# Float32 mixer and MoE layer: convolution sums in PSUM, low parts of weights on GpSimd, fewer native float32 chunks

## The chip, the core and the metric

The kernel runs on one core of one Trainium2 chip. The metric is device time in microseconds (us) of one execution. A core has five engines that the profile names PE (TensorE, matrix products), DVE (VectorE), ACT (ScalarE), POOL (GpSimd) and SP (SyncE, which here only issues DMAs). Every engine works through its own queue of instructions in order, and waits on semaphores for the others.

## The reference

One layer for a sequence of T = 256 tokens, D = 1024 channels, all float32. The first part mixes tokens, the second is a mixture of experts.

```
z = h @ w_in + b_in                        # 1024 x 6144: six blocks of 1024 columns
a_val, a_gate, sgu, g_a, g_b = split(z)    # sgu holds two blocks, u and v
ya = a_val * sigmoid(a_gate)
ya = causal_depthwise_conv(ya, 31 taps)    # every channel by itself
ya = silu(layer_norm(ya)) @ w_a + b_a
u, v = split(gelu(sgu))
yb = spatial_gating(u, layer_norm(v)) @ w_b + b_b
m  = sigmoid(g_a) * ya + sigmoid(g_b) * yb
out = m @ w_out + b_out                    # then residual, layer norm, modulation
y  = moe(h2)                               # top 4 of 32 experts, clamped SwiGLU, D -> 2*1024 -> D
```

The modulation rows (shift, scale, gate) come from c @ w_mod.

## The kernel before

**Part 1, the mixer (0 to about 316 us of the span).** Nine weight blocks of 1024 x 1024 go through PE one after the other: the block of a_gate, of a_val, V, U, G_b, G_a (columns of w_in), then w_b, w_a and w_out. A block is four chunks of 256 rows (one DMA of 1 MB each, issued by SP two chunks ahead), a chunk is two halves of 128 rows. A chunk is multiplied in one of two ways. A *native* chunk is multiplied as float32: 16 matmuls in the program, 32 in the trace. A *split* chunk is split into hi + lo: ACT casts the raw half to the rounded format fp32r (hi, L146), DVE subtracts (lo = raw - hi, L147), and PE multiplies hi by hi, hi by lo and lo by hi (L428 to L430): 48 matmuls. NAT_V, NAT_U, NAT_G, ... say which chunks of a block are native; N_LO = 6 buffers hold the lo halves of all blocks in turn.

**The convolution.** Each of the eight channel blocks n takes 31 taps. The first (L514) writes the product with its coefficient and the bias to cT[:, n] in SBUF, each of the other 30 (L516, SCALAR_TENSOR_TENSOR on 128 x 256 float32) reads that sum, adds one product and writes it back. That makes 248 DVE instructions. They are put into the background queue bgq in groups of four; bg_step (L408) takes groups out of it behind each chunk until their costs (0.33 each tap) have used a budget, BUD. Behind the convolution in the same queue stand the four steps of its layer norm (lna_mean, lna_var, lna_out twice: L600 to L617), whose result is split again (cahi, calo, L117/L118) and is the right-hand side of the w_a block.

**The order of the engines' queues.** Up to the chain behind w_out the framework's scheduler orders each engine's instructions by its own estimate of when they are ready, so that a budget or a cost that changes moves instructions. In the order that results DVE works on two channel blocks in turn, one tap of n, one of n + 1, as long as two are open.

**Around it.** macc and sacc (L250) are sums of modulation rows on DVE. sgb (L627) is the gate times the result of the w_b block, read from PSUM. The w_out block and its chain (L749 on: residual, layer norm, router, selection) lead to **part 2, the MoE**: 30 jobs, each an expert's weights streamed once.

**PSUM.** [...] The pool big holds three tiles of two banks, msp two of one.

Of the kernel before, what the change touches and what calls it, by code (L numbers as in the profile page):

```python
# [68 lines left out]
BUD = (7.2, 2.2)  # L69
# [6 lines left out]
def kernel(ctx, tc, a, out):  # L76
# [27 lines left out]
    def BIG():  # L104
        return big.tile([P, D], F32, name=nm("big"), tag="big")
# [60 lines left out]
    def push_block(key, w, c0, native):  # L166
        seq[key] = len(chunks)
        for ci in range(4):
            chunks.append(Chunk(lambda ci=ci: load_rows2(w, c0, ci), ci in native))

    for b, nat in ((1, ()), (0, ()), (3, NAT_V), (2, NAT_U), (5, NAT_G), (4, NAT_G)):
        push_block(("in", b), a["w_in"][0], b * D, nat)
    push_block("b", a["w_b"][0], 0, NAT_B)
    push_block("a", a["w_a"][0], 0, NAT_A)
    push_block("out", a["w_out"][0], 0, NAT_O)
# [173 lines left out]
    xT = [BIG(), BIG()]  # L349
# [6 lines left out]
    with tc.manual_schedule(engines={ET.DVE}):  # L356
# [23 lines left out]
        for g in range(2):  # L380
            pcol = MS()
            for w in range(2):
                for i in range(4):
# [4 lines left out]
            k4 = slice(g * 4, g * 4 + 4)
            ve.tensor_tensor(mcol[:, g, 0], pv[:, 0], par[:, k4, C_MOD], op=ALU.add)
            ve.scalar_tensor_tensor(mcol[:, g, 1], pv[:, 1], 1.0, par[:, k4, C_MOD + 1], op0=ALU.add, op1=ALU.add)  # L390
            for i in range(4):
                k = g * 4 + i
                src = xT[g][:, i * T:(i + 1) * T]
# [20 lines left out]
    def gemm_T(base, af, ahi, alo):  # L414
        accs = [BIG(), BIG()]
        for ci in range(4):
            ck = chunk(base + ci)
            for k2 in range(2):
                k = 2 * ci + k2
                for n in range(KC):  # L420
                    o = accs[n // 4][:, (n % 4) * T:(n % 4 + 1) * T]
# [86 lines left out]

    cT = sg

    def conv(n, t0, t1):
# [858 lines left out]
    undone = []  # L1370
    for j in range(NSTATIC + 1):
# [132 lines left out]
```

## Time and profile before

| | us |
|---|---|
| median of 3 runs | 1273.22 (1271.09 to 1273.25) |
| profiled execution | 1268.86 |
| its span, first to last instruction | 1267.0 |
| PE busy in the span | 1123.8 (89%) |
| DVE busy | 484.7 (38%) |
| ACT busy | 205.7 (16%) |
| POOL busy | 55.5 (4%) |
| DMA, mean over the span | 354 GB/s |

Times in rows are microseconds from the start of the span, and the name of an operation's tile says whose result it is: a name before the arrow is written, those behind it are read. A row with a count (x19) is a run of equal instructions, and its length goes from the first one's start to the last one's end. An instruction's record lasts somewhat longer than the distance to the next one, since they overlap. In brackets stands how long the engine was idle before, and whose work it waited for.

### The profile page before, as it was taken

What the parts mean: (1) busy time and instruction counts of PE and PEld (TensorE: products, weight loads), DVE (VectorE), ACT (ScalarE), POOL (GpSimd) and SP (SyncE); (2) the same over time, 40 slices, a digit from 0 to 9 for tenths busy, and PEclk for the clock granted to TensorE, in tenths of its full rate; (3) what the DMA queues carried; (4) which work ended last, traced back from release to release, by engine and by line L of the source; (5) the groups of instructions that cost most, each with busy time, mean ns of one, the idle gap of its engine ahead of it and who ended that gap; (6) DMA issues with size and microseconds to landing.
All of it is one profiled execution on the core that took longest, in us unless ns stands there. A gap on an engine that the chain in (4) does not pass through costs nothing. (4 is left out here: it accounts for less than half of the span.)

```text
span 1267.0 us, 14367 instructions
## 1 busy us (share of the span) xinstructions
PE 1123.8 (89%) x5454; PEld 548.3 (43%) x5454; DVE 484.7 (38%) x926; ACT 205.7 (16%) x344; POOL 55.5 (4%) x185
## 2 busy tenths in 40 slices
PE   1999999998999989999997999899888986998672
PEld 1998898876434334324331343334222321332110
DVE  6799999976321410321222113121121211132124
ACT  1533234533202001000110020011000100011000
POOL 6000000000200001000010010000000000000000
PEclk9999999999999999999998999899889988999676
DMA  9984346685897998999999999999999999999993
GB/s 367 368 334 134 116 151 223 231 306 204 349 418 293 383 418 330 375 399 404 377 417 417 417 403 404 416 417 416 416 417 417 416 417 418 417 417 417 417 414 111
DMA packets 84312, 449.13 MB, mean 354 GB/s; under 512 B 7377, under 2 KB 7417, under 8 KB 51424
## 3 DMA queue, kind: packets, MB, share of 16 engines
q1 hardware_dynamic: 82672, 443.84, 87.8%
q0 software_dynamic: 1552, 4.15, 0.9%
q8 instruction: 50, 0.82, 0.3%
q14 instruction: 38, 0.31, 0.1%
HBM read 446.92 MB, written 1.05 MB: 354 GB/s over the span
## 5 line engine op out<-in xcount | busy, mean ns | idle before, releaser
L1138 PE MATMUL big<-raw,S 128*32 128x512 f32 (+1 forms) x1600 | 279.0, 631 | 30.3 <-DMA raw<-in_w_gu_dram 30.3
L1149 PE MATMUL big<-raw,S 128*128 128x512 f32 x384 | 172.2, 602 | 0.0
L1314 DVE TENSOR_TENSOR ob<-big,g2c 64x512 f32<-64x512 f32 x48 | 33.0, 688 | 361.8 <-PE big L1289 253.1
L1138 PEld LDWEIGHTS big<-raw,S 128*32 128x32 f32 (+1 forms) x1600 | 63.3, 122 | 202.7 <-issue 128.8
L1149 PEld LDWEIGHTS big<-raw,S 128*128 128x128 f32 x384 | 71.9, 192 | 90.4 <-issue 89.3
L1289 PE MATMUL big<-raw,aT 128*32 128x512 f32 x512 | 75.9, 706 | 30.5 <-DMA raw<-in_w_dn_dram 29.2
L516 DVE SCALAR_TENSOR_TENSOR sg<-ya,par,sg 128x256 f32<-128x256 f32 x240 | 100.0, 470 | 0.6
L1280 PE MATMUL big<-raw,aT 128*128 128x512 f32 x192 | 87.0, 601 | 0.9 <-DMA raw<-in_w_dn_dram 0.9
L426 PE MATMUL big<-hT,raw 128*128 128x256 f32 x384 | 85.5, 379 | 0.0
L1342 PE MATMUL ms<-ob,ohT 128*128 128x512 f32 x144 | 76.8, 640 | 5.9 <-DVE gt L1182 3.2
L1334 DVE TENSOR_TENSOR y<-y,ms 128x512 f32<-128x512 f32 x72 | 48.9, 685 | 81.8 <-PE ms L1342 81.7
L426 PEld LDWEIGHTS big<-hT,raw 128*128 128x128 f32 x384 | 71.9, 190 | 9.5 <-issue 0.5
L1138 PE MATMUL big<-raw,aT 128*64 128x512 f32 x256 | 65.1, 621 | 4.2 <-DMA raw<-in_w_dn_dram 4.1
L147 DVE TENSOR_TENSOR lo<-raw,hi 128x1024 fp32r<-128x1024 f32 x46 | 55.2, 1216 | 9.5 <-ACT hi L146 6.4
L1172 ACT COPY g<-big 128x512 f32<-128x512 f32 x16 | 9.4, 585 | 302.1 <-PE big L1138 302.1
L1280 PEld LDWEIGHTS big<-raw,aT 128*128 128x128 f32 x192 | 35.2, 190 | 52.4 <-issue 50.6
L146 ACT CAST hi<-raw 128x1024 fp32r<-128x1024 f32 x46 | 46.3, 1051 | 59.1 <-DMA raw<-in_w_in_dram 17.3
L430 PE MATMUL big<-hThi,lo 128*128 128x256 f32 x192 | 55.0, 288 | 0.8 <-DVE lo L147 0.8
L428 PE MATMUL big<-hThi,hi 128*128 128x256 f32 x192 | 55.7, 291 | 0.0
L429 PE MATMUL big<-hTlo,hi 128*128 128x256 f32 x192 | 55.0, 287 | 0.1
L1289 PEld LDWEIGHTS big<-raw,aT 128*32 128x32 f32 x512 | 13.9, 118 | 87.5 <-DMA raw<-in_w_dn_dram 59.3
L1182 DVE TENSOR_TENSOR gt<-ms,bcols 128x256 f32<-128x256 f32 (+1 forms) x46 | 22.6, 491 | 75.0 <-PE ms L1208 75.0
(327 smaller groups left out, 1185.5 us busy)
## 6 DMA issues: line engine op xcount, KB each, us to landing
raw<-in_w_gu_dram SPq DMA_DIRECT2D x240, 1024.0 KB, 17.2
raw<-in_w_dn_dram SPq DMA_DIRECT2D x120, 1024.0 KB, 16.6
raw<-in_w_mod_dram SPq DMA_DIRECT2D x24, 1024.0 KB, 7.6
raw<-in_w_in_dram SPq DMA_DIRECT2D x24, 1024.0 KB, 7.1
raw<-in_w_b_dram SPq DMA_DIRECT2D x4, 1024.0 KB, 5.0
raw<-in_w_a_dram SPq DMA_DIRECT2D x4, 1024.0 KB, 5.0
raw<-in_w_out_dram SPq DMA_DIRECT2D x4, 1024.0 KB, 9.0
x<-in_x_dram SPq DMA_DIRECT2D x1, 1024.0 KB, 8.3
```

The costliest lines, as they stand in the source:

```text
L147: ve.tensor_tensor(c.lo[q], src, f(c.hi[q]), op=ALU.subtract)
L426: pe.matmul(o, lhsT=ck.raw[:, k2 * D + n * P:k2 * D + (n + 1) * P], rhs=af[:, k], start=b0, stop=b1)
L428: pe.matmul(o, lhsT=ck.hi[k2][:, s], rhs=ahi[:, k], start=b0, stop=False)
L429: pe.matmul(o, lhsT=ck.hi[k2][:, s], rhs=alo[:, k], start=False, stop=False)
L430: pe.matmul(o, lhsT=ck.lo[k2][:, s], rhs=ahi[:, k], start=False, stop=b1)
L516: ve.scalar_tensor_tensor(cT[:, n], ya[:, n, t:t + T], bcol(n, t), cT[:, n], op0=ALU.mult, op1=ALU.add)
L1138: pe.matmul(out_[q * n:(q + 1) * n], lhsT=S, rhs=raw[:, w0(q):w0(q) + 512], start=first_, stop=last_)
L1149: pe.matmul(job.ps[h][:, n * 512:(n + 1) * 512], lhsT=S[:, k, 0:P], rhs=raw[:, h * D + n * 512:h * D + (n + 1) * 512], start=f0, stop=f1)
L1280: pe.matmul(job.pd[0][:, n * 512:(n + 1) * 512], lhsT=job.aT[:, k, 0:P], rhs=raw[:, k2 * D + n * 512:k2 * D + (n + 1) * 512], start=f0, st ...
L1289: pe.matmul(job.pd[0][q * 32:(q + 1) * 32, 0:512], lhsT=job.aT[:, k, 0:32], rhs=raw[:, k2 * D + h * 512:k2 * D + (h + 1) * 512], start=ci ...
L1334: ve.tensor_tensor(yy, yy, box[0], op=ALU.add)
L1342: pe.matmul(box[0], lhsT=w()[r, t * P:(t + 1) * P], rhs=o(n)[r], start=i == 0, stop=i == len(parts_) - 1)
```

## The change

1. Of V, U, G_b and G_a one chunk each stays native (chunk 1), where three were: eight chunks more are split.
2. The lo halves of V, U, G_b, G_a and w_b are subtracted by GpSimd. Those of the first two blocks, of w_a and of w_out stay on DVE.
3. The sums of the convolution stand in a PSUM tile csum of one bank, [128, 2, 256]: channel block n uses half n % 2. After tap 31 ACT copies the half to cT in SBUF (L528).
4. Part 1 uses five single banks (zbp), one for csum and two of msp; the pool big is opened before the MoE.
5. The budget is three numbers, the cost of a tap 0.4.
6. The second half of the gate row's sum is added right before the MoE, and no longer in its first units.

Line numbers move: taps L514/L516 to L524/L526, lo L147 to L153, hi L146 to L152, sgb L627 to L639, modulation sums L250 to L257, layer norm L603 to L615.

```
-NAT_V = (1, 2, 3)
-NAT_U = (1, 2, 3)
-NAT_G = (0, 1, 3)
+NAT_V = (1,)
+NAT_U = (1,)
+NAT_G = (1,)
...
-BUD = (7.2, 2.2)
+BUD = (6.6, 5.0, 2.2)
...
-    big = ctx.enter_context(tc.tile_pool(name="big", bufs=3, space=PSUM))
     msp = ctx.enter_context(tc.tile_pool(name="msp", bufs=2, space=PSUM))
+    banks = ctx.enter_context(ExitStack())
+    zbp = banks.enter_context(tc.tile_pool(name="zbp", bufs=5, space=PSUM))
+    cvp = banks.enter_context(tc.tile_pool(name="cvp", bufs=1, space=PSUM))
...
-        ve.tensor_tensor(c.lo[q], src, f(c.hi[q]), op=ALU.subtract)
+        c.eng.tensor_tensor(c.lo[q], src, f(c.hi[q]), op=ALU.subtract)
...
+    for b, nat, eng in ((1, (), ve), (0, (), ve), (3, NAT_V, gp), (2, NAT_U, gp), (5, NAT_G, gp), (4, NAT_G, gp)):
+        push_block(("in", b), a["w_in"][0], b * D, nat, eng)
+    push_block("b", a["w_b"][0], 0, NAT_B, gp)
+    push_block("a", a["w_a"][0], 0, NAT_A, ve)
+    push_block("out", a["w_out"][0], 0, NAT_O, ve)
...
     def gemm_T(base, af, ahi, alo):
-        accs = [BIG(), BIG()]
+        accs = [ZB() for i in range(4)]
...
-            bg_step(BUD[0] if ck.native else BUD[1])
+            bg_step(BUD[0] if ck.native else BUD[1] if ck.eng is gp else BUD[2])
...
     cT = sg
+    csum = cvp.tile([P, 2, T], F32, name="csum")
 
     def conv(n, t0, t1):
         for t in range(t0, t1):
+            o = csum[:, n % 2]
             if t == 0:
-                ve.tensor_scalar(cT[:, n], ya[:, n, 0:T], bcol(n, 0), bcol(n, C_CONVB), op0=ALU.mult, op1=ALU.add)
+                ve.tensor_scalar(o, ya[:, n, 0:T], bcol(n, 0), bcol(n, C_CONVB), op0=ALU.mult, op1=ALU.add)
             else:
-                ve.scalar_tensor_tensor(cT[:, n], ya[:, n, t:t + T], bcol(n, t), cT[:, n], op0=ALU.mult, op1=ALU.add)
+                ve.scalar_tensor_tensor(o, ya[:, n, t:t + T], bcol(n, t), o, op0=ALU.mult, op1=ALU.add)
+            if t == TAPS - 1:
+                sc.copy(cT[:, n], o)
...
+    for n in range(2):
+        ns = slice(n * 512, (n + 1) * 512)
+        ve.tensor_tensor(g2c[:, ns], g2c[:, ns], pg2[n], op=ALU.add)
+    banks.close()
+    bigs.append(ctx.enter_context(tc.tile_pool(name="big", bufs=3, space=PSUM)))
...
-    def gate_unit():
-        return [lambda: ve.tensor_tensor(g2c, g2c, pg2, op=ALU.add)]
```

At the start of the convolution DVE's queue reads so before; ya is the gated input, macc a modulation sum, sg_604 the sums:

```order
L507 SCALAR_TENSOR_TENSOR ya<-big_614,par,sg_604 128x256 x4
L514 TENSOR_SCALAR sg_604<-ya,par 128x256
L250 SCALAR_TENSOR_TENSOR macc_415<-raw_848,condT,macc_415 128x2048
L516 SCALAR_TENSOR_TENSOR sg_604<-ya,par,sg_604 128x256
L514 TENSOR_SCALAR sg_604<-ya,par 128x256
L516 SCALAR_TENSOR_TENSOR sg_604<-ya,par,sg_604 128x256 x19
```

Two first taps stand almost side by side there, so two channel blocks are open. In the changed kernel the queue of the same place (bs_899 is a bias row of the spatial gating) reads:

```order
L524 TENSOR_SCALAR csum<-ya,par 128x256
L526 SCALAR_TENSOR_TENSOR csum<-ya,par,csum 128x256
L257 SCALAR_TENSOR_TENSOR macc_422<-raw_857,condT,macc_422 128x2048
L526 SCALAR_TENSOR_TENSOR csum<-ya,par,csum 128x256 x17
L552 SCALAR_TENSOR_TENSOR bs_899<-ms_901,par,bs_899 128x128 x4
L552 SCALAR_TENSOR_TENSOR bs_899<-ms_907,par,bs_899 128x128 x4
L526 SCALAR_TENSOR_TENSOR csum<-ya,par,csum 128x256 x12
L524 TENSOR_SCALAR csum<-ya,par 128x256
L526 SCALAR_TENSOR_TENSOR csum<-ya,par,csum 128x256 x13
```

There 30 taps stand between one first tap (L524) and the next: one channel block is open at a time, all through the convolution.

At the convolution's end DVE's queue reads so before; lo_18.. are halves of w_a, ms_1804 the mean of the layer norm, sgb the gate times the w_b block:

```order
L147 TENSOR_TENSOR lo_1889<-raw_1886,hi_1888 128x1024
L516 SCALAR_TENSOR_TENSOR sg_604<-ya,par,sg_604 128x256 x4
L147 TENSOR_TENSOR lo_1893<-raw_1886,hi_1892 128x1024
L516 SCALAR_TENSOR_TENSOR sg_604<-ya,par,sg_604 128x256
L250 SCALAR_TENSOR_TENSOR sacc_2096<-raw_2099,condT,sacc_2096 128x1024
L603 TENSOR_TENSOR sg_604<-sg_604,ms_1804 128x1024 x2
L147 TENSOR_TENSOR lo_1954<-raw_1951,hi_1953 128x1024
```

In the changed kernel the last part of the convolution, from the last sgb on, reads:

```order
L639 SCALAR_TENSOR_TENSOR sgb_1812<-zb_2093,par,sgb_1812 128x256
L526 SCALAR_TENSOR_TENSOR csum<-ya,par,csum 128x256
L153 TENSOR_TENSOR lo_2397<-raw_2390,hi_2396 128x1024
L526 SCALAR_TENSOR_TENSOR csum<-ya,par,csum 128x256
L257 SCALAR_TENSOR_TENSOR sacc_2448<-raw_2513,condT,sacc_2448 128x1024
```

and its very end:

```order
L257 SCALAR_TENSOR_TENSOR sacc_2448<-raw_2629,condT,sacc_2448 128x1024
L526 SCALAR_TENSOR_TENSOR csum<-ya,par,csum 128x256 x10
L524 TENSOR_SCALAR csum<-ya,par 128x256
L526 SCALAR_TENSOR_TENSOR csum<-ya,par,csum 128x256 x30
L615 TENSOR_TENSOR sg_611<-sg_611,ms_2152 128x1024 x2
```

The eight sgb, which stood behind the layer norm before, now stand between taps with the last 60 of the 248 taps behind the first of them, and all eight sums of sacc and six low halves of w_a stand ahead of the last tap, where one macc and four halves of w_a stood.

## Rows read from the trace of the kernel before

**Rows 1.** The page's costliest group: xcount | busy us, mean ns | idle, releaser.

```profile
L1138 PE MATMUL big<-raw,S 128*32 128x512 f32 (+1 forms) x1600 | 279.0, 631 | 30.3 <-DMA raw<-in_w_gu_dram 30.3
```

**Rows 2.** Windows: length, busy PE, PEld, DVE, ACT, POOL, PEclk, DMA, GB/s.

```profile
39.05:43.67 4.62, 4.56 (x20) 4.27 (x21) 4.62 (x8) 4.48 (x7) 0.00 (x0) 1.00 1.04 376
43.67:48.29 4.62, 4.62 (x42) 4.62 (x42) 4.62 (x7) 2.35 (x5) 0.00 (x0) 1.00 0.94 335
125.00:150.00 25.00, 25.00 (x123) 22.19 (x122) 25.00 (x65) 6.70 (x12) 0.00 (x0) 1.00 0.38 119
350.00:375.00 25.00, 25.00 (x98) 9.81 (x96) 8.79 (x18) 1.84 (x3) 0.00 (x0) 1.00 1.01 418
```

**Rows 3.** PE timeline: start us, length us, operation, xcount [idle before <-releaser].

```profile
125.18 20.88 PE L426 MATMUL big<-hT,raw 128*128 128x256 f32 x96
...
238.24 1.98 PE L492 MATMUL big<-bg,ones 1*128 1x512 f32 x4
...
244.47 0.39 PE L429 MATMUL big<-calo,hi 128*128 128x256 f32 x1 [0.39 <-DVE calo L118]
...
266.13 1.45 PE L473 MATMUL ms<-sacc,ones 128*128 128x512 f32 x3
...
282.97 1.04 PE L671 MATMUL ms<-ident,sc 128*128 128x128 f32 x8
...
286.53 0.48 PE L694 MATMUL big<-hi,mhi 128*128 128x512 f32 x1
```

**Rows 4.** DVE timeline, the convolution's start and its end.

```profile
83.94 3.22 DVE L507 SCALAR_TENSOR_TENSOR ya<-big,par,sg 128x256 f32<-128x256 f32 x8 [2.10 <-PE big L430]
...
90.38 7.60 DVE L516 SCALAR_TENSOR_TENSOR sg<-ya,par,sg 128x256 f32<-128x256 f32 x19
...
208.34 5.15 DVE L516 SCALAR_TENSOR_TENSOR sg<-ya,par,sg 128x256 f32<-128x256 f32 x10
...
224.18 0.48 DVE L516 SCALAR_TENSOR_TENSOR sg<-ya,par,sg 128x256 f32<-128x256 f32 x1
224.58 1.28 DVE L250 SCALAR_TENSOR_TENSOR sacc<-raw,condT,sacc 128x1024 f32<-128x1024 f32 x1
```

**Rows 5.** One DVE group: line, op, tiles, shapes, xcount | busy, mean ns.

```profile
L572 DVE SCALAR_TENSOR_TENSOR m<-ms,par,bs 128x256 f32<-128x256 f32 x8 | 3.7, 466 | 0.0
```

**Rows 6.** DVE timeline, the layer norm behind the convolution.

```profile
232.76 1.23 DVE L147 TENSOR_TENSOR lo<-raw,hi 128x1024 fp32r<-128x1024 f32 x1 [2.31 <-PE big L430]
233.91 1.75 DVE L611 RECIPROCAL rstd<-rstd 128x256 f32<-128x256 f32 x1
235.57 1.18 DVE L147 TENSOR_TENSOR lo<-raw,hi 128x1024 fp32r<-128x1024 f32 x1
...
238.93 3.22 DVE L627 SCALAR_TENSOR_TENSOR sgb<-big,par,sgb 128x256 f32<-128x256 f32 x8
...
243.20 1.22 DVE L118 TENSOR_TENSOR calo<-sg,cahi 128x1024 fp32r<-128x1024 f32 x1
```

**Rows 7.** ACT timeline, the layer norm behind the convolution.

```profile
231.98 0.48 ACT L610 ACTIVATE rstd<-ms,eps 128x256 f32<-128x256 f32 x1 [1.47 <-PE ms L609]
...
240.39 1.03 ACT L117 CAST cahi<-sg 128x1024 fp32r<-128x1024 f32 x1
```

**Rows 8.** POOL groups by form, whole span.

```profile
L925 POOL TENSOR_SCALAR oh<-iota_s,P 128x32 fp32r<-128x32 f32 x32 | 11.1, 366 | 264.7 <-PE ms L948 262.8 <-DVE P L903 1.9
L925 POOL TENSOR_SCALAR oh<-iota_s,P 128x128 fp32r<-128x128 f32 x10 | 6.1, 613 | 0.0
...
L464 POOL MEMSET sacc<- 128x1024 f32 x1 | 1.0, 959 | 61.5 <-PE ms L569 61.5
...
L295 POOL TENSOR_SCALAR lowr<-pio 128x1 f32<-128x1 f32 x1 | 0.2, 233 | 0.0
```

**Rows 9.** Timeline at the start of the span, DVE and POOL.

```profile
15.21 9.51 DVE L250 SCALAR_TENSOR_TENSOR macc<-raw,condT,macc 128x2048 f32<-128x2048 f32 x4
15.30 2.35 POOL L297 TENSOR_SCALAR lowr<-tgt 128x1 f32<-128x1 f32 x1
```

More of the change, by code (lines that the diff above doesn't have):

```diff
@@ L104, in BIG, with ZB @@
     def BIG():
-        return big.tile([P, D], F32, name=nm("big"), tag="big")
+        return bigs[0].tile([P, D], F32, name=nm("big"), tag="big")
+    def ZB():
+        return zbp.tile([P, 512], F32, name=nm("zb"), tag="zb")
     def MS():
@@ L133, with __init__ @@
     class Chunk:
-        def __init__(self, load, native):
-            self.load, self.native = load, native
+        def __init__(self, load, native, eng):
+            self.load, self.native, self.eng = load, native, eng
             self.raw, self.hi, self.lo = None, [], []
@@ L164, with push_block @@
     seq = {}
-    def push_block(key, w, c0, native):
+    def push_block(key, w, c0, native, eng):
         seq[key] = len(chunks)
         for ci in range(4):
[L169 to L175, printed above, removed]
+            chunks.append(Chunk(lambda ci=ci: load_rows2(w, c0, ci), ci in native, eng))
+    for b, nat, eng in ((1, (), ve), (0, (), ve), (3, NAT_V, gp), (2, NAT_U, gp), (5, NAT_G, gp), (4, NAT_G, gp)):
[3 more added lines that the diff above has]
+    push_block("out", a["w_out"][0], 0, NAT_O, ve)
     regs = {}
@@ L347, in part_of @@
         return t_.rearrange("p (w c) -> p w c", w=2)[:, :, g * 512:(g + 1) * 512]
-    xT = [BIG(), BIG()]
+    xT = [ZB() for i in range(4)]
     mcol = const.tile([P, 2, 2, 4], F32, name="mcol")
@@ L392 @@
                 k = g * 4 + i
-                src = xT[g][:, i * T:(i + 1) * T]
+                src = xT[k // 2][:, i % 2 * T:(i % 2 + 1) * T]
                 scale, shift = mcol[:, g, 1, i:i + 1], mcol[:, g, 0, i:i + 1]
@@ L420, in gemm_T @@
                 for n in range(KC):
-                    o = accs[n // 4][:, (n % 4) * T:(n % 4 + 1) * T]
+                    o = accs[n // 2][:, (n % 2) * T:(n % 2 + 1) * T]
                     s = slice(n * P, (n + 1) * P)
@@ L430, in gemm_T @@
                         pe.matmul(o, lhsT=ck.lo[k2][:, s], rhs=ahi[:, k], start=False, stop=b1)
-            bg_step(BUD[0] if ck.native else BUD[1])
-        return [accs[n // 4][:, (n % 4) * T:(n % 4 + 1) * T] for n in range(KC)]
+            bg_step(BUD[0] if ck.native else BUD[1] if ck.eng is gp else BUD[2])
+        return [accs[n // 2][:, (n % 2) * T:(n % 2 + 1) * T] for n in range(KC)]
     def z_block(b):
@@ L476, in mod_g2 @@
     def mod_g2(c0, c1):
-        pg = BIG()
+        pg = [ZB(), ZB()]
         steps = []
@@ L491, in step @@
         def step(i, lhsT, w, n):
-            pe.matmul(pg[:, n * 512:(n + 1) * 512], lhsT=lhsT, rhs=w, start=i < 2, stop=i >= len(steps) - 2)
+            pe.matmul(pg[n], lhsT=lhsT, rhs=w, start=i < 2, stop=i >= len(steps) - 2)
         return [lambda i=i, s=s: step(i, *s) for i, s in enumerate(steps)], pg
@@ L520 @@
             t1 = min(t0 + 4, TAPS)
-            bgq.append((0.33 * (t1 - t0), lambda n=n, t0=t0, t1=t1: conv(n, t0, t1)))
+            bgq.append((0.4 * (t1 - t0), lambda n=n, t0=t0, t1=t1: conv(n, t0, t1)))
     wsr = A8([P, KC, P], name="wsr")
@@ L631 @@
         fn()
-    sc.copy(g2c, pg)
+    for n in range(2):
+        sc.copy(g2c[:, n * 512:(n + 1) * 512], pg[n])
     z = gemm_T(seq["a"], cT, ca_hi, ca_lo)
@@ L679, in prepare_router @@
             sc.mul(wr[:, k], wr[:, k], modc[:, 0, k:k + 1])
-    yo = [BIG(), BIG()]
+    yo = [[ZB(), ZB()] for t in range(NT)]
     def out_mm(t, ci, k2, n):
@@ L687, in out_mm @@
         k = 2 * ci + k2
-        o = yo[t][:, n * 512:(n + 1) * 512]
+        o = yo[t][n]
         s = slice(n * 512, (n + 1) * 512)
@@ L835 @@
     c_norm(0)
-    pl = BIG()
+    pl = ZB()
     c_transpose(0)
@@ L897 @@
     c_lo(1, 0)
-    pj = BIG()
+    pj = ZB()
     for t in range(NT):
@@ L930 @@
     c_lo(1, 1)
+    for n in range(2):
+        ns = slice(n * 512, (n + 1) * 512)
+        ve.tensor_tensor(g2c[:, ns], g2c[:, ns], pg2[n], op=ALU.add)
+    banks.close()
+    bigs.append(ctx.enter_context(tc.tile_pool(name="big", bufs=3, space=PSUM)))
     class Job:
@@ L1376 @@
         else:
-            waiting += [tail_unit(), bias_unit(0), bias_unit(1), weight_unit(), gate_unit()] + start_units()
+            waiting += [tail_unit(), bias_unit(0), bias_unit(1), weight_unit()] + start_units()
             first_gather = gather(0)
```

5 lines of the change are left out of this document (3 added, 2 removed).

## The prediction

> **What bounds the kernel now.** I read busy time by stretch first, then the timelines of PE and DVE where part 1 ends, then the costliest groups. From 350 to 375 us the DMA queues are busy all the time at 418 GB/s [rows 2], and PE's costliest group, in the MoE, is idle 30.3 us waiting for weights [rows 1]. The MoE is thus a stream of fixed length that starts when part 1 hands over; what part 1 wins or loses goes into the total about one for one. In part 1 PE and DVE are both full: 125 to 150 us has 25.00 us of each [rows 2], and neither can be relieved alone. Where they meet is the w_a block. It starts at 244.47 after a wait for DVE's calo and runs to 266.13 [rows 3]; calo comes from the layer norm, and that from the last tap, which stands at 224.18 and ends, by the start of the next instruction, at 224.58 [rows 4]. So the question is when, in the changed kernel, the last tap ends. I call that time E.
>
> **PE's side.** 96 matmuls (three native chunks) take 20.88 us [rows 3], 6.96 each. The w_a block has four split chunks, of which 190 of 192 matmuls stand between 244.47 and 266.13 [rows 3]: 5.47 a chunk. Eight chunks that change from one to the other save 8 x 1.49 = 11.9 us of PE. Where does that put the end of w_b? The blocks V to w_b start when a_val's does not hold PE any more, at 83.9 [rows 4], and w_b ended at 238.2, where the next work of PE starts [rows 3]: 154.3 us, of which 12 x 6.96 + 8 x 5.47 = 127.3 are chunks and 27.0 other work and waits. Of these I drop 12 (an estimate: the 32 small matmuls of the layer norm, now behind w_b, and waits for DVE's low halves). New: 4 x 6.96 + 16 x 5.47 = 115.4, plus 15, so w_b ends at about 214.
>
> **DVE's side, taken away.** 12 of the 16 low halves that stood between 83.9 and E leave DVE. One takes 1.15 us (232.76 to 233.91 [rows 6]): -13.8.
>
> **DVE's side, added.** Two more halves of w_a stand ahead of E (+2.3), eight sums sacc at 1.2 (the first at 224.58 has 1.28, the next starts a little before it ends [rows 4]; +9.6) and eight sgb, 3.22 together [rows 6]. Then the taps themselves. Each tap reads the sum that the tap before wrote. With two channel blocks in turn, 19 taps took 7.60 us, a distance of (7.60 - 0.48)/18 = 0.396; where one block alone was left, ten took 5.15, a distance of 0.52 [rows 4]. So a tap that directly follows the tap it depends on pays 0.124 us. In the changed order only one block is open at a time. The reason is csum: two blocks have two halves, but the first tap of the next block also waits for ACT's copy of the last one. I count 188 taps right behind their predecessor, where some 17 were: 171 x 0.124 = +21.2. This is the largest term, and rests on the delay being the same for a sum in PSUM, which no row shows. Bounds: nothing at all (0.396, PSUM hides it) and twice the delay (0.64); I take the row's 0.52. The seven changes of block wait for an ACT copy: an ACT operation of that size out of PSUM takes 0.48 [rows 7]; with both semaphores 0.6, six times beyond what other work covers, +3.6 (0 to 8, when ACT is in the middle of a 1.03 us cast [rows 7]). The sum is +26.1: by its own work DVE would reach E at 224.6 + 26.1 = 250.7.
>
> A PSUM operand as such costs nothing that rows show: the taps' 0.48 in SBUF [rows 4] stands beside 466 ns for an operation of the same kind and size that reads PSUM [rows 5]. [...]
>
> **What PE adds to this.** The first sgb reads w_b's result, so it can't start before 214, and behind it stand 60 taps, 44 of them chained: 44 x 0.52 + 16 x 0.396 + 8 sgb (3.2) + 6 sacc (7.2) + one half (1.15) + one change (0.6) = 41.4. So E is at least about 255, and the two ways agree to 5 us: PE ends w_b early, stands idle for about 42 us, and waits for DVE. I take 254, that is 29.4 us later than before.
>
> **GpSimd's low halves.** 32 halves, 128 x 1024, two inputs. GpSimd's one-hot takes 366 ns at 32 columns and 613 at 128 [rows 8]: 2.57 ns a column, 2.9 us a half. Bounds: a MEMSET of that size, 0.96 [rows 8], and twice the slope for two inputs, 5.7. A block has six halves, 17.4 us against 23.4 of PE (6.96 + 3 x 5.47), so PE doesn't wait until a half takes 3.9.
>
> **DVE and GpSimd beside each other.** While DVE ran 2048-column sums with two SBUF inputs back to back, a GpSimd operation on one column took 2.35 us, the length of one such sum [rows 9], and 0.23 for the same operation elsewhere [rows 8]. GpSimd thus waits for DVE; the other direction has no row. Some 11 instructions of DVE with two SBUF inputs stand among GpSimd's halves. If each waits half a half (1.45) with GpSimd busy three quarters of the time, that is 12 us on DVE's side; all of GpSimd's halves in a bad order could make it 20. DVE has about 4 us to spare against the 214 of w_b, so between 0 and 16 reach E; I take 6, near half. The taps themselves have one SBUF input now. [...]
>
> **From E to the end.** Before, 244.47 - 224.58 = 19.9 us lay between E and w_a. Two low halves stood ahead of the reciprocal and behind it; without them the reciprocal starts at 232.5, when the root is there [rows 7], not at 233.9, and the next step 1.1 us sooner [rows 6]. calo could follow ACT's cast, at 241.4 [rows 7], not at 243.2, behind the sgb and a half [rows 6]. That is 1.4 + 1.1 + 1.8 = 4.3, less 0.9 for small ACT copies that are ordered between: -3.4. So w_a starts at 254 + 16.5 = 270.5, 26.0 later. PE then comes from idleness: in its first 4.62 us of work it did 20 matmuls, in the next 42, with a granted clock of 1.00 in both records [rows 2]; half of 4.62 is lost, +2.3. The transposes and small matmuls between the two halves of w_out (282.97 to 286.53 [rows 3]) fall into PE's idle time now: -3.6. The sum of the gate row's second half adds 0.3 on DVE ahead of the MoE, and three matmuls of the modulation right behind w_a (L473, 1.45 [rows 3]) move ahead of it, which gives back 0.4, since DVE works there anyway. PSUM in single banks and the budgets cost nothing by themselves: they act through the order.
>
> **Sum.** +26.0 + 2.3 - 3.6 + 0.3 - 0.4 + 6 = +30.6 on the profiled execution's 1268.86, so 1299.5. The median of the runs is 4.4 us above that execution; so 1303 against 1273.22. The 11.9 us that PE saves are in none of these terms, because PE waits.
>
> **Rivals.**
> 1. *The chain's delay is hidden in PSUM* (0.396 everywhere). For it: nothing in the rows but that the store is another. DVE then reaches the first sgb before w_b ends, and E is 214 + 41.4 - 44 x 0.124 = 250, later if ports cost; the rest stays: about 10 us less, 1293. Chance 0.13.
> 2. *PSUM makes the chain longer* (0.64). E moves by 188 x 0.12 = 22, of which 4 were to spare: about 1320. For it: the sum goes out to another memory and comes back; against it: reading PSUM cost nothing extra [rows 5]. [...] Chance 0.12.
> 3. *GpSimd starves PE*, at 4.6 us a half or more. The six halves of each of four blocks (27.6 against 23.4) and eight of w_b (36.8 against 22) then put w_b's end some 30 us later, and the sgb with it: 1330 to 1345. [...] Chance 0.05.
> 4. *Faster.* If the last tap came before 229, w_a would start where it did, and PE's savings would show: all of the 11.9, about 1262. It needs at most some 15 us of DVE work behind w_b's end; the order has 41. It could come about only if taps in PSUM were far shorter than 0.396, about half. Chance 0.04.
> The forecast itself gets 0.66.
>
> **How the numbers follow.** The range goes from 1286, the rival with the hidden chain where the ports cost nothing, to 1320, the longer chain; outside stay rival 3, rival 4 and the far ends, under 2 in 10. A measurement of this kernel can tell 0.2% (2.5 us) from no change. Faster 0.05 (rival 4 and a little), within 0.2% 0.02, slower 0.93.
>
> **What would show it.** In the profile after: taps in rows of 30 at about 0.52 each; DVE busy without a break from 84 to about 254, PE idle for 35 to 45 us ahead of w_a with calo or the sums as releaser; w_a's first matmul near 270 (with the ports' 6, 276); GpSimd's halves near 2.9 us; the MoE unchanged in length. I am wrong if taps go at 0.40, if PE waits for lo inside V to w_b, or if w_a starts before 250.

## The result and the profile after

The changed kernel takes 1307.43 us (1305.15 to 1309.92, 4 runs), the kernel before 1272.15 in the same comparison: 1.0285 times as long, 95% interval 1.0266 to 1.0303. The forecast was 1303, range 1286 to 1320. The profiled execution took 1309.92 us, its span 1308.2.

First VectorE's timeline of the changed kernel, from the convolution to the layer norm behind it (columns as in [rows 4]):

```profile
105.47 2.16 DVE L552 SCALAR_TENSOR_TENSOR bs<-ms,par,bs 128x128 f32<-128x128 f32 x8 [3.88 <-DMA bs<-in_b_s_dram]
...
114.25 0.55 DVE L524 TENSOR_SCALAR csum<-ya,par 128x256 f32<-128x256 f32 x1 [0.44 <-ACT sg L528]
...
126.92 1.94 DVE L333 TENSOR_SCALAR vt<-vt,mv,rs 128x1024 f32<-128x1024 f32 x1
...
129.18 0.80 DVE L333 TENSOR_SCALAR vt<-vt,mv,rs 128x1024 f32<-128x1024 f32 x1
...
154.29 2.78 DVE L124 TENSOR_TENSOR sblo<-uT,sbhi 128x512 fp32r<-128x512 f32 x1
...
158.81 0.69 DVE L124 TENSOR_TENSOR sblo<-uT,sbhi 128x512 fp32r<-128x512 f32 x1
...
177.67 15.72 DVE L526 SCALAR_TENSOR_TENSOR csum<-ya,par,csum 128x256 f32<-128x256 f32 x30
...
206.93 1.23 DVE L153 TENSOR_TENSOR lo<-raw,hi 128x1024 fp32r<-128x1024 f32 x1 [0.24 <-PE zb L437]
...
209.99 1.28 DVE L257 SCALAR_TENSOR_TENSOR sacc<-raw,condT,sacc 128x1024 f32<-128x1024 f32 x1 [1.43 <-DMA raw<-in_w_mod_dram]
...
221.31 0.48 DVE L639 SCALAR_TENSOR_TENSOR sgb<-zb,par,sgb 128x256 f32<-128x256 f32 x1
...
235.64 1.28 DVE L257 SCALAR_TENSOR_TENSOR sacc<-raw,condT,sacc 128x1024 f32<-128x1024 f32 x1 [3.28 <-DMA raw<-in_w_mod_dram]
...
250.46 15.72 DVE L526 SCALAR_TENSOR_TENSOR csum<-ya,par,csum 128x256 f32<-128x256 f32 x30
267.89 2.35 DVE L615 TENSOR_TENSOR sg<-sg,ms 128x1024 f32<-128x1024 f32 x2 [1.71 <-PE ms L612]
276.01 1.75 DVE L623 RECIPROCAL rstd<-rstd 128x256 f32<-128x256 f32 x1 [5.76 <-ACT rstd L622]
```

Thirty taps in a row take 15.72 us, (15.72 - 0.48)/29 = 0.526 each, where [rows 4] had 0.396 with two blocks in turn and 0.52 with one. The last tap ends the row that begins at 250.46, so it ends at 266.1; before it was 224.6. At 206.93 and 221.31 DVE and PE meet: the low half waits 0.24 us for PE, and the first sgb doesn't wait at all. So it is DVE's own work that sets when the last tap ends.

The busy time by stretch over that end (columns as in [rows 2]):

```profile
225.00:250.00 25.00, 5.09 (x9) 1.84 (x7) 20.79 (x36) 2.59 (x4) 0.53 (x1) 0.58 0.65 231
250.00:275.00 25.00, 7.08 (x19) 4.89 (x20) 17.48 (x33) 3.77 (x4) 0.00 (x0) 0.53 0.03 10
275.00:300.00 25.00, 21.21 (x143) 18.98 (x142) 12.61 (x10) 14.54 (x26) 1.63 (x2) 0.86 0.28 90
```

PE, nearly full in part 1 before (24.61 of the 25 us from 225 to 250, at a granted clock of 1.00), works 5.09 and 7.08 us of 25. The granted clock in its records there is 0.58 and 0.53.

PE's timeline in the same place shows who it waits for:

```profile
222.68 1.12 PE L499 MATMUL zb<-bg,ones 1*128 1x512 f32 x2
...
249.90 1.22 PE L612 MATMUL ms<-sg,onesD 128*128 128x256 f32 x2 [19.91 <-ACT sg L528]
266.63 1.22 PE L612 MATMUL ms<-sg,onesD 128*128 128x256 f32 x2 [15.52 <-ACT sg L528]
270.26 5.21 PE L621 MATMUL ms<-sq,onesD 128*128 128x256 f32 x16 [2.40 <-ACT sq L616]
...
284.12 1.22 PE L435 MATMUL zb<-cahi,hi 128*128 128x256 f32 x4 [2.40 <-ACT cahi L123]
285.38 0.58 PE L436 MATMUL zb<-calo,hi 128*128 128x256 f32 x1
```

w_b ends at 222.7, where L499 starts (before: 238.2 [rows 3]). PE then waits 19.91 and 15.52 us for sums of the convolution. The 16 matmuls of the variance take 5.21 us, at a granted clock of 0.71 on average, and w_a's first product with calo, which is what [rows 3] shows at 244.47, comes at 285.38: 40.9 us later.

### The profile page after: what moved, and what is told of

It reads as the page before. It is cut to its first block, busy times and chain, and to the rows that moved or that the text cites. A ratio compares the mean times of both kernels' runs of the same rounds, so it can differ in the third digit from the quotient of the medians.

```text
span 1308.2 us, 14718 instructions
## 1 busy us (share of the span) xinstructions
PE 1123.6 (86%) x5582; PEld 548.2 (42%) x5582; DVE 489.1 (37%) x911; ACT 223.6 (17%) x369; POOL 130.3 (10%) x217
## 5 line engine op out<-in xcount | busy, mean ns | idle before, releaser
L526 DVE SCALAR_TENSOR_TENSOR csum<-ya,par,csum 128x256 f32<-128x256 f32 x240 | 117.2, 488 | 6.8
L435 PE MATMUL zb<-hThi,hi 128*128 128x256 f32 x320 | 91.3, 287 | 0.0
L436 PE MATMUL zb<-hTlo,hi 128*128 128x256 f32 x320 | 90.8, 284 | 0.3 <-DVE hTlo L124 0.3
L437 PE MATMUL zb<-hThi,lo 128*128 128x256 f32 x320 | 90.1, 283 | 0.0
L153 POOL TENSOR_TENSOR lo<-raw,hi 128x1024 fp32r<-128x1024 f32 x32 | 76.9, 2411 | 90.4 <-ACT hi L152 54.8
L152 ACT CAST hi<-raw 128x1024 fp32r<-128x1024 f32 x62 | 63.9, 1055 | 77.7 <-PE zb L436 45.0
L938 POOL TENSOR_SCALAR oh<-iota_s,P 128x32 fp32r<-128x32 f32 (+2 forms) x56 | 22.8, 431 | 396.1 <-PE ms L966 394.3
L435 PEld LDWEIGHTS zb<-hThi,hi 128*128 128x128 f32 x320 | 61.5, 193 | 0.2
L436 PEld LDWEIGHTS zb<-hTlo,hi 128*128 128x128 f32 x320 | 61.2, 191 | 0.7 <-DVE hTlo L124 0.6
L437 PEld LDWEIGHTS zb<-hThi,lo 128*128 128x128 f32 x320 | 61.1, 191 | 0.0
```

The source lines that it names most:

```text
L153: c.eng.tensor_tensor(c.lo[q], src, f(c.hi[q]), op=ALU.subtract)
L435: pe.matmul(o, lhsT=ck.hi[k2][:, s], rhs=ahi[:, k], start=b0, stop=False)
L436: pe.matmul(o, lhsT=ck.hi[k2][:, s], rhs=alo[:, k], start=False, stop=False)
L437: pe.matmul(o, lhsT=ck.lo[k2][:, s], rhs=ahi[:, k], start=False, stop=b1)
L526: ve.scalar_tensor_tensor(o, ya[:, n, t:t + T], bcol(n, t), o, op0=ALU.mult, op1=ALU.add)
```

## The experiments

All times are medians, compared with the kernel before on the same chip. The end of the last tap and the first product of w_a with calo are read from each profiled execution as above.

| kernel | us | ratio to before (95%) | last tap ends | w_a's calo product |
|---|---|---|---|---|
| before | 1272.15 | | 224.6 | 244.5 |
| changed | 1307.43 | 1.0285 (1.0266 to 1.0303) | 266.1 | 285.4 |
| 1: two banks | 1280.99 | 1.0062 (1.0035 to 1.0089) | 233.0 | 255.7 |
| 2: sums in SBUF | 1320.16 | 1.0370 (1.0340 to 1.0401) | 269.0 | 296.3 |
| 3: PSUM sums alone | 1318.10 | 1.0362 (1.0331 to 1.0392) | 276.1 | 295.3 |
| 4: GpSimd halves alone | 1288.22 | 1.0137 (1.0101 to 1.0173) | 230.1 | 261.2 |
| 5: one bank, no copy | 1302.81 | 1.0255 (1.0236 to 1.0275) | 260.3 | 279.4 |
| 6: two banks, no copy | 1278.35 | 1.0055 (1.0036 to 1.0074) | 235.1 | 252.7 |
| 7: two banks, halves on VectorE | 1303.61 | 1.0259 (1.0240 to 1.0277) | 262.5 | 283.1 |
| 8: two native chunks | 1283.74 | 1.0094 (1.0067 to 1.0122) | 233.0 | 258.2 |
| 9: gate product from PSUM | 1276.60 | 1.0029 (1.0013 to 1.0046) | 230.0 | 251.2 |
| 10: no native chunk | 1277.78 | 1.0029 (1.0009 to 1.0049) | 219.7 | 244.5 |
| 11: fewer native alone | 1298.94 | 1.0209 (1.0178 to 1.0241) | 248.8 | 269.0 |
| 12: sums behind the norm | 1268.45 | 0.9963 (0.9947 to 0.9979) | 216.9 | 237.4 |

**1. Two banks for the sums.**

```
-    zbp = banks.enter_context(tc.tile_pool(name="zbp", bufs=5, space=PSUM))
-    cvp = banks.enter_context(tc.tile_pool(name="cvp", bufs=1, space=PSUM))
+    zbp = banks.enter_context(tc.tile_pool(name="zbp", bufs=4, space=PSUM))
+    cvp = banks.enter_context(tc.tile_pool(name="cvp", bufs=2, space=PSUM))
...
-    csum = cvp.tile([P, 2, T], F32, name="csum")
+    csum = [cvp.tile([P, 512], F32, name="csum", tag="cs") for i in range(2)]
...
-            o = csum[:, n % 2]
+            o = csum[n % 2][:, :T]
```

> The changed kernel, but the sums of the convolution stand in two PSUM tiles of one bank each, taken in turn, instead of two halves of one bank (part 1 then has four single banks for the products). Theory (one open chain): the cause of the loss is that a next channel block has to wait for ScalarE's copy of the last, so that each tap directly follows the one it depends on at 0.52 us. Then two blocks are open here, taps go at 0.40, the last tap comes at about 229 to 233 us instead of 266, PE doesn't stand idle for more than 15 us ahead of w_a, and the time is 1262 to 1280. Rival (PSUM sums as such are slow): taps stay at 0.5 or above with two blocks in turn, and the time stays above 1295. Rival (GpSimd's low halves hold VectorE up): also above 1295, with taps at 0.40 and waits around GpSimd's instructions. Third possibility: with four banks instead of five PE waits for a bank at each block, which adds some 1 us for each of seven blocks.

Measured: 1280.99 us. VectorE's timeline of this kernel:

```profile
106.80 14.97 DVE L526 SCALAR_TENSOR_TENSOR csum<-ya,par,csum 128x256 f32<-128x256 f32 x38
...
153.88 0.55 DVE L524 TENSOR_SCALAR csum<-ya,par 128x256 f32<-128x256 f32 x1 [2.96 <-ACT sg L528]
...
203.81 0.55 DVE L524 TENSOR_SCALAR csum<-ya,par 128x256 f32<-128x256 f32 x1 [3.90 <-ACT sg L528]
...
232.59 0.48 DVE L526 SCALAR_TENSOR_TENSOR csum<-ya,par,csum 128x256 f32<-128x256 f32 x1
```

Two blocks are open, 38 taps take 14.97 us, 0.392 each, with their sums in PSUM. So a PSUM sum is no slower than one in SBUF (0.396), and the chain of one open block was what cost: 26 us of the change's 35 go with this edit. The time is 1 us above the upper end of the theory's range. In this trace VectorE still waits 2.96 and 3.90 us for ScalarE's copies, which the sixth experiment takes away, and PE waits 5.3 us once for a bank that a gate of ScalarE reads, which fits the third possibility.

**2. Sums back in SBUF, the rest of the change kept.**

```
-            o = csum[:, n % 2]
+            o = cT[:, n]
...
-            if t == TAPS - 1:
-                sc.copy(cT[:, n], o)
```

> The changed kernel, but the sums of the convolution stay in SBUF as before, without the copies; GpSimd's low halves and the fewer native chunks remain. If the sums in PSUM are the only cause of the loss, then two blocks are open, taps go at 0.40, the last tap comes before 222 us and the time is about 1260 to 1268. Rival (two SBUF inputs against GpSimd): each tap now has two SBUF inputs, and in the changed kernel a subtraction of 0.69 us on VectorE took 2.78 beside a GpSimd half; if each of the 32 halves of 2.4 us stops VectorE for its length, up to 77 us are lost among the taps, the last tap comes at 260 to 290 and the time is 1300 to 1335. In the trace that would be taps of up to 2.8 us, and GpSimd's halves longer than 2.4.

Measured: 1320.16 us, the rival. VectorE's timeline:

```profile
198.78 27.98 DVE L524 SCALAR_TENSOR_TENSOR sg<-ya,par,sg 128x256 f32<-128x256 f32 x38
226.68 2.49 DVE L522 TENSOR_SCALAR sg<-ya,par 128x256 f32<-128x256 f32 x1
```

one long low half, and one tap of the row of 38 with the half beside it, from the timeline of both engines:

```profile
165.00 13.12 POOL L152 TENSOR_TENSOR lo<-raw,hi 128x1024 fp32r<-128x1024 f32 x1 [7.51 <-PE zb L436]
...
200.16 2.55 POOL L152 TENSOR_TENSOR lo<-raw,hi 128x1024 fp32r<-128x1024 f32 x1 [4.95 <-issue]
200.36 2.62 DVE L524 SCALAR_TENSOR_TENSOR sg<-ya,par,sg 128x256 f32<-128x256 f32 x1
```

and GpSimd's low halves in the groups by form:

```profile
L152 POOL TENSOR_TENSOR lo<-raw,hi 128x1024 fp32r<-128x1024 f32 x32 | 108.3, 3401 | 83.7 <-ACT hi L151 57.4 <-PE zb L436 16.9 <-issue 6.0
```

38 taps that take 14.97 us in the first experiment take 27.98 here, and a low half 3.40 us on average instead of the 2.39 that the changed kernel shows below. Six of the 38 make the difference: each lasts some 2.6 us beside a half, the others 0.47 to 0.48. Over the whole convolution 24 instructions of it are held like that, some 49 us together. Three of them are first taps, a TENSOR_SCALAR with one SBUF input (2.49 us at 226.68, 0.40 in the kernel before). The other way round a half that meets a row of taps can wait through many of them: most last 2.3 to 2.8 us, one 13.12. That is what the sums in PSUM avoided. The eleventh experiment has as many split chunks and its sums in SBUF too, but the halves on VectorE (and the budgets and PSUM pools of before): it takes 1298.94 us. As far as the two compare, GpSimd's halves beside sums in SBUF cost more than they relieve.

**3. The sums in one PSUM bank alone** (the changed kernel with all low halves on VectorE, three native chunks, the old budgets and tap cost).

```
-NAT_V = (1,)
-NAT_U = (1,)
-NAT_G = (1,)
+NAT_V = (1, 2, 3)
+NAT_U = (1, 2, 3)
+NAT_G = (0, 1, 3)
...
-    push_block("b", a["w_b"][0], 0, NAT_B, gp)
+    push_block("b", a["w_b"][0], 0, NAT_B, ve)
```

> Only the sums of the convolution in one PSUM bank (with the copies, the single banks and the later gate sum): low halves back on VectorE, three native chunks a block as before, budgets and tap cost as before. Theory (one open chain): +21 us for chained taps, +4 for the turns from block to block, and sums and gates ordered ahead of the last tap put it at about 260 to 270 us; the time is 1300 to 1320, about as slow as the whole change. Rival (the other two parts made the loss): 1268 to 1278.

Measured: 1318.10 us. VectorE's timeline, the last channel block:

```profile
259.89 0.55 DVE L524 TENSOR_SCALAR csum<-ya,par 128x256 f32<-128x256 f32 x1 [0.44 <-ACT sg L528]
260.47 15.71 DVE L526 SCALAR_TENSOR_TENSOR csum<-ya,par,csum 128x256 f32<-128x256 f32 x30
```

The first tap waits for ScalarE, and thirty taps take 15.71 us, as in the changed kernel. The last tap, at 276.1, comes later than the 260 to 270 that were expected; the time lies in the range. The sums in one bank, with the order that comes with them, cost more alone than the whole change.

**4. GpSimd's halves alone**, on the kernel before.

```
-        ve.tensor_tensor(c.lo[q], src, f(c.hi[q]), op=ALU.subtract)
+        c.eng.tensor_tensor(c.lo[q], src, f(c.hi[q]), op=ALU.subtract)
```

with c.eng GpSimd for V, U, G_b, G_a and w_b.

> The kernel before with one edit: the low halves of V, U, G_b, G_a and w_b (16 halves) on GpSimd. Sums in SBUF, three native chunks a block. If GpSimd's halves stop taps with two SBUF inputs for their whole length, 16 x 2.4 = 38 us are lost on VectorE where 16 x 1.15 = 18 are won, the last tap comes some 10 to 25 us later and the time is 1280 to 1297. If they don't, VectorE wins up to 14 us, w_a then waits for w_b's end at 238 us instead, and the time is 1266 to 1272.

Measured: 1288.22 us, the branch with the waits. VectorE's timeline:

```profile
203.04 27.10 DVE L516 SCALAR_TENSOR_TENSOR sg<-ya,par,sg 128x256 f32<-128x256 f32 x35
```

35 taps that would take some 14 us two blocks in turn take 27.10. Five of them last 2.44 to 2.61 us instead of 0.48, which is 10 of the 13 us. The last tap ends only 5.5 us later than before, less than expected; but w_a comes 16.7 later, and PE waited 10.06 us for a bank that ScalarE had yet to read.

**5. One bank, no copy.**

```
-                ve.scalar_tensor_tensor(o, ya[:, n, t:t + T], bcol(n, t), o, ...)
-            if t == TAPS - 1:
-                sc.copy(cT[:, n], o)
+                ve.scalar_tensor_tensor(cT[:, n] if t == TAPS - 1 else o, ya[:, n, t:t + T], bcol(n, t), o, ...)
```

> The changed kernel, sums in one PSUM bank, but the last tap of each channel block writes straight to SBUF, so ScalarE's eight copies are gone. In the program the first tap of the next block then waits for VectorE's own last tap of the block before, because both halves lie in one bank. If the shared bank is what keeps one block open at a time, taps stay at 0.52 us, only the turns from block to block (0.4 to 1.2 us each) go, and the time is 1295 to 1305. If ScalarE's copy is what does it (as the prediction put it), two blocks are open, taps go at 0.40 and the time is 1265 to 1282.

Measured: 1302.81 us. VectorE's timeline, the last channel block:

```profile
244.10 0.55 DVE L524 TENSOR_SCALAR csum<-ya,par 128x256 f32<-128x256 f32 x1
244.69 15.19 DVE L526 SCALAR_TENSOR_TENSOR csum<-ya,par,csum 128x256 f32<-128x256 f32 x29
```

Nothing waits for ScalarE any more, and still 29 taps take 15.19 us, 0.525 each. So the copy isn't what keeps one block open; the csum tile in one bank is. In the program the first tap of a block waits for VectorE's last tap of the block before in the same bank, though it writes another half. No run here shows that the hardware needs this wait: it is an order that the framework sets. Whether it goes by the bank or by the tile isn't separated, since no run has two tiles in one bank; in SBUF two slices of one tile are open side by side [rows 4].

**6. Two banks, no copy, the bias of the spatial gating loaded earlier.** The first and the fifth experiment's edits, and the load of bs ahead of a_val's block.

> Two PSUM banks for the sums as in the first experiment, the last tap of each block written straight to SBUF, and the load of the spatial gating's bias issued earlier. In the first experiment VectorE waited 7.3 us for ScalarE's copies and 4.4 for that bias, but PE ended w_b only at 227.4, with seven taps and eight gates behind it. If VectorE still sets the last tap, all 11.7 us come back: 1268 to 1271. If w_b's end on PE (held up by four banks) and the layer norm set it, 3 to 6 us come back: 1274 to 1279.

Measured: 1278.35 us, the second branch: between medians 2.6 us come back and not 11.7, and the intervals of the two ratios overlap, so even these aren't sure. The last tap comes 2.1 us later than in the first experiment, and the stretch from it to w_a is 5.1 shorter. All engines' timelines around 170 us:

```profile
167.78 7.03 POOL L153 TENSOR_TENSOR lo<-raw,hi 128x1024 fp32r<-128x1024 f32 x3
...
168.51 6.86 DVE L587 TENSOR_TENSOR uT<-uT,m 128x512 f32<-128x512 f32 x1
...
175.46 0.62 ACT L123 CAST sbhi<-uT 128x512 fp32r<-128x512 f32 x1 [7.94 <-DVE uT L587]
...
178.33 3.03 ACT L594 ACTIVATE sgb<-zb,par 128x256 f32<-128x256 f32 x8
...
179.22 0.58 PE L435 MATMUL zb<-hThi,hi 128*128 128x256 f32 x1 [6.64 <-ACT sgb L594]
```

GpSimd does three low halves back to back. VectorE's product of u and the mixed value, two SBUF inputs, 0.68 us elsewhere, starts 0.73 us behind the first of them and ends 0.56 us behind the last. ScalarE's cast waits 7.94 us for it, its gate stands behind the cast, and PE waits 6.64 us for the bank that the gate reads.

**7. Two banks, low halves on VectorE.** The first experiment with ve for gp in the blocks.

> The first experiment (two banks) with all low halves back on VectorE. About 30 halves of 1.15 us, 34 us, come to VectorE ahead of the last tap; what it loses to GpSimd's halves in the first experiment (single instructions of 1.8 to 4.6 us where 0.7 to 0.8 is their length, some 8 us together) goes. If VectorE sets the last tap, the time is 1298 to 1310; if PE does, it stays at 1281.

Measured: 1303.61 us; VectorE sets the last tap. So once two blocks are open, GpSimd's halves are worth 22.6 us (1303.61 - 1280.99). With the engine the budget behind a split chunk of these blocks changes too, from 5.0 to 2.2 (see BUD in the change); what that does by itself wasn't tried.

**8. Two native chunks in each of the four blocks**, otherwise the sixth.

> The two banks without copies as in the sixth experiment, but two native chunks in V, U, G_b and G_a each instead of one. PE works 4 x 1.49 = 6 us more ahead of w_b's end, GpSimd has eight halves fewer. If PE's work sets w_b's end, the time is 4 to 7 us above that experiment's; if GpSimd's halves do (waits of PE for them, or of VectorE beside them), it is the same or up to 5 us below.

Measured: 1283.74 us, 5.4 above the sixth, the branch in which PE's work sets w_b's end. It fits 4 x 1.49; as the four times go from 1280.65 to 1287.54, it doesn't show that figure to the microsecond.

**9. The gate's product reads PSUM.**

```
-        m2 = tmp.tile([P, 512], F32, name=nm("m2"), tag="m2")
+        m2 = ps
```

> The sixth experiment, with the spatial gating's mixed value left in PSUM, so that its product with u has one SBUF input instead of two. In the sixth experiment one such product lasted 6.86 us instead of 0.68, while GpSimd did three low halves back to back; ScalarE's cast and its gate waited behind it, and PE stood 6.6 us for a free bank. If two SBUF inputs are what makes VectorE wait for GpSimd, these four products last 0.7 us each, PE's wait at 179 us shrinks below 2 us, and the time is 1270 to 1274. If something else held that instruction, the time stays at 1278.

Measured: 1276.60 us. The product and the subtraction behind it, and PE's wait:

```profile
167.62 0.68 DVE L587 TENSOR_TENSOR uT<-uT,ms 128x512 f32<-128x512 f32 x1
...
168.61 4.06 DVE L124 TENSOR_TENSOR sblo<-uT,sbhi 128x512 fp32r<-128x512 f32 x2
...
174.94 0.38 PE L435 MATMUL zb<-hThi,hi 128*128 128x256 f32 x1 [2.14 <-ACT sgb L594]
```

The product is back at 0.68 us. The four products take 0.678 us on average here (0.678 and 0.680 in the tenth and twelfth experiments), 2.225 in the sixth, which fits the second SBUF input as what held them; but in the eighth, with that input and eight GpSimd halves fewer, they take 0.678 as well, and no row here shows where the halves stood beside them. The two subtractions behind the last product (uT and sbhi, both in SBUF) now wait instead, 4.06 us for two, and PE still waits 2.14. The product's wait is gone; the gain, 1.8 us between medians, is less than expected, and the intervals of the two ratios overlap.

**10. No native chunk in the four blocks**, otherwise the ninth.

> The ninth experiment with no native chunk in V, U, G_b and G_a. PE has 4 x 1.49 = 6 us less ahead of w_b's end; GpSimd has eight halves more, 8 x 2.4 = 19.2 us a block against 21.9 of PE. If PE's own work sets w_b's end, the time is 4 to 6 us below the ninth experiment's: 1264 to 1269, below the kernel before. If GpSimd's halves or VectorE's taps set it, it is the same or up to 6 us above.

Measured: 1277.78 us, no gain, though the last tap ends 10.3 us sooner. VectorE's timeline ahead of w_a, and PE's wait:

```profile
240.72 2.60 DVE L257 SCALAR_TENSOR_TENSOR sacc<-raw,condT,sacc 128x1024 f32<-128x1024 f32 x2 [2.06 <-DMA raw<-in_w_mod_dram]
243.24 1.22 DVE L124 TENSOR_TENSOR calo<-sg,cahi 128x1024 fp32r<-128x1024 f32 x1
...
244.51 0.58 PE L436 MATMUL zb<-calo,hi 128*128 128x256 f32 x1 [2.66 <-DVE calo L124]
```

The norm's result waits behind two modulation sums, which wait 2.06 us for their DMA; the stretch from the last tap to w_a takes 24.8 us. And w_a's calo product comes when it came before the change, but the time stays 4 us (by the ratio) to 6 (by the medians) above that of the kernel before. The profiled execution, with 1272.81 us one of the shorter of the twelve, doesn't show where they lie. That is open.

**11. Fewer native chunks alone**, on the kernel before.

> The kernel before with one edit: one native chunk instead of three in V, U, G_b and G_a, low halves on VectorE, sums in SBUF. PE saves 11.9 us, VectorE gets 16 halves of 1.15 us, 18.4. If VectorE's last tap sets the start of w_a, the time is 1284 to 1294; if PE's work does, 1260 to 1264.

Measured: 1298.94 us, on VectorE's side but 5 us above the range: gates and sums were ordered ahead of the last tap here as well, which the expectation left out.

**12. The modulation sums behind w_a**, otherwise the tenth.

```
-    bgq += [(2.3, lambda ci=ci: mod_sc2_add(ci)) for ci in range(4)] + [(0.0, mod_sc2_fin)]
...
     z = gemm_T(seq["a"], cT, ca_hi, ca_lo)
+    bgq += [(2.3, lambda ci=ci: mod_sc2_add(ci)) for ci in range(4)] + [(0.0, mod_sc2_fin)]
```

> The tenth experiment, with the eight modulation sums (sacc) put behind the w_a block in the program, so that only one of them stands ahead of the first calo in VectorE's order, where six did. In the tenth experiment w_a's second product waited 2.66 us for calo, which stood behind a sum that waited for its DMA, and the last tap ended 24.8 us ahead of it, where the kernel before has 19.9. If these sums are what keeps that stretch long, it shrinks to 17 to 20 us and the time falls by 4 to 8 us, to 1269 to 1274: at last no slower than the kernel before. If the sums only move into the w_out block's path, which VectorE also serves, the time stays at 1278.

Measured: 1268.45 us, 0.9963 times the kernel before (0.9947 to 0.9979): the only version that beats both, and half a microsecond below the range. The first calo and the product that waits for it:

```profile
236.16 1.23 DVE L124 TENSOR_TENSOR calo<-sg,cahi 128x1024 fp32r<-128x1024 f32 x1 [2.29 <-ACT cahi L123]
...
237.44 0.58 PE L436 MATMUL zb<-calo,hi 128*128 128x256 f32 x1 [0.25 <-DVE calo L124]
```

calo now waits for ScalarE's cast, not for a sum. The stretch from the last tap to w_a is 20.5 us instead of 24.8, the last tap itself comes 2.8 sooner than in the tenth, and w_a's product comes at 237.44, 7.0 us sooner than before the change. The median is only 4.3 us below that of the kernel before (1272.72 on this chip), so not all of the 7.0 reaches the end.

## Why the prediction was right

- **The open chain.** Right in size: 0.526 measured, 0.52 taken. The rival with hidden delay and the one with a longer chain are both out, by the changed kernel's trace and by the first experiment. The reason that the prediction gave was only half right: it put it on the first tap's wait for ScalarE's copy, and the fifth experiment shows that the one-bank tile does it without the copy. Without the copies the time is 1302.8, with two banks and the copies 1281.0.
- **PSUM operands.** VectorE's groups by form in the changed kernel:

```profile
L526 DVE SCALAR_TENSOR_TENSOR csum<-ya,par,csum 128x256 f32<-128x256 f32 x240 | 117.2, 488 | 6.8
...
L524 DVE TENSOR_SCALAR csum<-ya,par 128x256 f32<-128x256 f32 x8 | 4.4, 546 | 3.4 <-ACT sg L528 3.4
```

  Its 488 ns hold the chained taps. With two blocks in turn the same tap takes 0.48 in the timeline of the first experiment, as in [rows 4], so the taps show no extra time for a sum in PSUM. The first tap, which writes PSUM from SBUF, is longer, 546 ns against 0.40 us before, but there are eight.
- **The last tap.** 254 + 6 = 260 predicted, 266.1 measured: both ways to it were longer. On PE, w_b ended at 222.7 and not 214: of the 27.0 us of other work the prediction dropped 12, and 138.7 - 115.4 = 23.3 remained, so only some 4 went. In part that is because 12 of the 16 matmuls of the mean still stood ahead of it, and because a split chunk of these blocks takes about 5.7 us (matmuls 0.119 apart from 184 to 201 us) where w_a's rows gave 5.47. But the first sgb waited for nothing, so VectorE's own way set the last tap, predicted at 250.7 + 6 = 256.7. On it stood waits for DMA that were in none of the terms: 3.88 us for the bias row, where it waited 2.27 for PE before, and 1.43 and 3.28 for modulation sums. A second macc sum stood behind 84 us (2.3), the taps together took some 2 us more than their term, and the first taps, which had no term, some 2 us more than before. Behind the first sgb stood 44.8 us (221.3 to 266.1), predicted 41.4; there the wait of 3.28 explains the difference.
- **The turns between blocks.** Five cost 0.44 us of waiting and one 1.20, together 3.4; predicted 3.6, in which 0.12 us a turn for semaphores was the author's estimate and in no row.
- **GpSimd.** 2.39 us a half, predicted 2.9; its group in the changed kernel:

```profile
L153 POOL TENSOR_TENSOR lo<-raw,hi 128x1024 fp32r<-128x1024 f32 x31 | 73.9, 2391 | 47.1 <-PE zb L437 23.8 <-ACT hi L152 11.5 <-issue 7.3
```

  PE didn't wait for a half: its matmuls that read one (L437) show 0.0 us of idle time ahead of them. The 6 us taken for VectorE's waits beside GpSimd, which the prediction puts down to ports, were too much in this kernel: the subtraction at 154.29 lasted 2.78 us instead of 0.69, and the TENSOR_SCALAR at 126.92, which has one SBUF input, 1.94 instead of 0.80, together 3.2. The prediction looked at instructions with two SBUF inputs alone. The waits that it assumed are there, longer where GpSimd's halves stand back to back (6.86 us in the sixth experiment), and on both sides (2.78 us here, and 13.12 for a half in the second experiment). No run shows what in the hardware makes them.
- **From the last tap to w_a.** 16.5 predicted, 19.3 measured (266.1 to 285.4). The same matmuls in the kernel before:

```profile
224.72 0.70 PE L600 MATMUL ms<-sg,onesD 128*128 128x256 f32 x2 [0.32 <-DVE sg L516]
...
228.22 3.72 PE L609 MATMUL ms<-sq,onesD 128*128 128x256 f32 x16
```

  At a granted clock of 0.50 the last two of the mean took 1.22 us instead of 0.70, and at 0.71 on average the 16 of the variance 5.21 instead of 3.72 (1.00 in both places before), together 2.0 of the 2.8, and VectorE waited 5.76 us at the reciprocal. The prediction put the price of PE's idleness only behind w_a's start.
- **Behind w_a's start.** From its calo product to the first long run of the MoE's weight loads on SP it took 77.8 us before (244.5 to 322.3) and 73.9 after (285.4 to 359.3): 3.9 given back, predicted 1.4 in sum.
- **The sum.** The errors are +6.1 for the last tap, +2.8 for the stretch behind it and -2.5 behind w_a's start, 6.4 in all. The profiled execution, the longest of the four, stands 10.4 us above the 1299.5 forecast for it; the 4 us between that and the 6.4 lie in the MoE, and why is open. The median stands only 4.4 above the 1303 (the prediction's own sum gives 1303.8), and this is luck: the prediction took the median to lie 4.4 us above the profiled execution, as it did before, and it lies 2.5 below it.

## What to carry to other kernels

Where every instruction needs the result of the one before on its own engine, what counts is how many independent chains stand open (0.526 us a tap with one in the changed kernel, 0.392 with two in the first experiment), and with this framework a PSUM tile in one bank made one chain of two without any address in common (0.525 in the fifth experiment): give each chain a tile in a bank of its own, as the first experiment did. A relief for one engine is worth what the order behind the meeting point lets through; here each of the three parts alone made the kernel slower (1.014 to 1.036), and together with two banks, no copies, the gate's product from PSUM, the modulation sums moved behind and all chunks of the four blocks split they made it 0.4% faster. Before work goes to GpSimd, list VectorE's instructions with two SBUF inputs that stand beside it (2.78 us instead of 0.69 in the changed kernel), its TENSOR_SCALARs from SBUF to SBUF (1.94 instead of 0.80), and who waits for them (PE for 6.64 us in the sixth experiment).

## What was not expected of the hardware

- A VectorE instruction with two SBUF inputs waited for more than one GpSimd instruction: it lasted 6.86 us beside three halves that stood back to back and took 7.03 (sixth experiment).
- One SBUF input was enough: TENSOR_SCALARs from SBUF to SBUF lasted 1.94 us instead of 0.80 (changed kernel) and 2.49 instead of 0.40 (second experiment) beside a half.
- Both sides got longer, and the averages hide how: with two SBUF inputs in the taps (second experiment) GpSimd's halves went from 2.39 to 3.40 us on average, but most stayed under 2.8 and one took 13.12; the taps went to (27.98 - 0.48)/37 = 0.74 between starts, but six of 38 took 2.6 and the rest 0.47 to 0.48.
